# Where a diffusion backbone's modulation products run: other stages of a two-layer kernel, one pass for the context, and two steps of side work a piece at two places

## The chip, the cores and the metric

The kernel runs on one core of one Trainium2 chip. A core has engines that run side by side: TensorE (PE: matmuls, with its weight loads as PEld), VectorE (DVE), ScalarE (ACT), GpSimd (POOL) and SyncE (SP), which here only issues transfers. Transfers run on 16 DMA engines. The metric is the device time of one execution in microseconds; lower is better.

## What is computed

Two layers over 256 latent tokens (x) and 256 context tokens (ctx), width 1024, fp32. The core of the reference, cut:

```python
mod   = silu(c) @ w_mod[l] + b_mod[l]          # latents
mod_c = silu(c_ctx) @ w_mod[l] + b_mod[l]      # context
sh1, sc1, ga1, sh2, sc2, ga2 = split(mod, 6)   # and the same six of mod_c
h  = rms_norm(x, g_pre_mix[l]) * (1 + sc1) + sh1      # hc from xc with mod_c
(mq, mk, mv, mo, mg, aq, ak, av, nq, nk, nv, zg) = split(h @ w_in[l])   # and from hc
y_ml = mlstm_branch(...)     # both directions, starts from the context's state
y_ga = gqa_latent(...)       # rotary, keys of context and latents
y_na = na_latent(...)        # neighbourhood window, plus the context
o = sum over branches of sigmoid(zg) * (y @ w_branch) @ w_out[l]
x = x + ga1 * rms_norm(o, g_post_mix[l])
f = conv_ffn(rms_norm(x, g_pre_ffn[l]) * (1 + sc2) + sh2, w_up, conv, w_down)
x = x + ga2 * rms_norm(f, g_post_ffn[l])
# in layer 0 the context takes the same path; in layer 1 it only gives keys, values and states
```

The six vectors sh1, sc1, ga1, sh2, sc2, ga2 are called keys below. In layer 0 each has two streams, latents and context; in layer 1 only sh1 and sc1 have both.

## The kernel before, in words

**Weights come in pieces.** The program is a list, `self.prog`, of pieces. A `Raw` is one transfer of 512 KB from memory into one of five raw tiles, issued on SP's queue in the order of use (`dma` in `run`, line 190); a raw tile comes free when its piece has been split or used. A weight piece is split before use (lines 208 and 209): ScalarE copies it to `whi` in a rounded format, VectorE subtracts to get `wlo`. `mm3` (line 307) then makes three matmuls, high by high, high by low, low by high. Splits run up to two pieces ahead. `block` cuts a projection into pieces of two 128-row slices (24 matmuls of 512 columns in layer 0; latents alone, in layer 1, take 24 of 256 or 12 of 512); `down_block` makes one-slice pieces for `w_out` and `w_down`.

**Side work.** Attention and mLSTM are Python generators in the queue `self.side`. After each piece `run` calls `step` as often as the piece's `side` says, once by default: a generator emits its instructions up to its next `yield`. So side work stands between weight pieces in every engine's order, and all engines execute in that order. `finish(key)` and `drain` emit, without pieces between, whatever a generator has left; a piece's `need` calls them where a result is wanted. The generators: `g_na` (neighbourhood attention; 14 steps in layer 0, 10 in layer 1), `g_gqa` (2 steps of tables and norms, 7 of rotary work, then 14 or 10 of attention), `g_gates` (5 steps), `g_mlstm` (2 steps, then four heads, each scores with the weighting product, an empty step and the outputs; it emits empty steps while the flags `mready` or `vready` are not set) and `g_mlfin` (waits for `oready`, then normalises the heads and transposes them, line 1075). In an attention step (`g_attend`) stand the PV product of the unit before last (line 701), the transposes of the last unit (687) and the scores of this one (648, 651), with VectorE's and ScalarE's softmax between.

**The order of a layer's mixer** (`layer`, line 1090 on): nq, in layer 1 the first NA gate, nk, nv, keys and values (kv), queries (q), the NA gates (in layer 1 the GA gates too), the NA projection (needs `na`), in layer 0 the GA gates, mk, in layer 0 the GA projection (needs `gqa`), mq, mv, in layer 1 the GA projection, the first ML gate, mo, the second ML gate, the ML projection (needs `drain`). Then `w_out`, norms, the FFN's eleven up blocks with convolution taps on VectorE (1308), and the down blocks.

**Modulation.** sc1 and sh1 of layer 0 are made by matmuls at the start. All other keys are made by `mod_dot` (line 424): each of eight pieces per key brings a transposed weight block of 128 outputs by 1024 inputs and VectorE multiplies it with the broadcast vector `CB` and sums along the row (line 440, `scalar_tensor_tensor` with `accum_out`). The latents take one operation over 1024 columns, which writes its products back over the raw tile. The context takes two over 512 columns, which write into the scratch tile `jnk` and leave two half sums to be added at the key's end (line 450). These pieces have `side=0`, no split and no matmul. `mod_end` adds the bias and gains. `spread` (line 482) puts such pieces at even distances among the pieces from a place to the program's end. Before, ga1, sh2, sc2, ga2 of layer 0 and sh1 of layer 1 (40 two-stream pieces) are spread over layer 0's mixer from nv on, and sc1, ga1, sh2, sc2, ga2 of layer 1 (8 two-stream and 32 one-stream pieces) over layer 0's FFN, ups from the third block on and both downs, 80 pieces. The dots between the first ML gate and the ML projection of layer 0 get `side=1`.

## Time and profile before

| | |
|---|---|
| median of 3 runs | 1533.33 us (1532.9 to 1535.78) |
| the profiled execution | 1536.47 us, of which the span is 1534.7 us |
| mean granted TensorE clock | 0.983 |
| busy: PE, PEld, DVE | 1451.6, 1251.6, 1089.4 us |
| busy: ACT, POOL | 731.4, 214.9 us |
| transfers | 238.08 MB, mean 155 GB/s |

The span is the time from the first to the last instruction. A group line of the profile names a source line, an engine, an operation and its tiles (out<-in), then count, busy time and mean duration. A waits line gives the total waiting time, how often, and the longest wait. A line of the timeline has start and duration in us and, in brackets, the idle time before it and what ended it. Matmuls overlap each other in the records, so a busy TensorE isn't TensorE at its peak: how many matmuls stand in a stretch tells more. Stages of the span: start to about 50 us, layer 0's mixer to about 570, `w_out` and norms to 661, ups to about 846, downs to about 973, layer 1's mixer to about 1310, then its FFN.

### The profile page before, as it was taken

Reading aid. Unit: us, or ns where it says so; the run is one execution under the profiler, and the core shown is the slowest. Engines: PE = TensorE matmul, PEld = TensorE weight load, DVE = VectorE, ACT = ScalarE, POOL = GpSimd, SP = SyncE. Lnnn points to the kernel's source line nnn. Section 1 sums busy time; section 2 is a strip of 40 time slices with the busy share of each in tenths; the row PEclk is TensorE's granted clock in tenths of the full one; section 3 lists DMA queues with packets and bytes.
Section 4 is the critical chain, followed back from the end, with each engine's and each line's share of the span. In section 5 each row is a group of like instructions: output and inputs, shape, how many; then the busy total and the mean of one; then the engine's idle time right before and its main releaser. Section 6 shows DMA issues by size and latency. Waiting matters only on the chain.

```text
span 1534.7 us, 23004 instructions
## 1 busy us (share of the span) xinstructions
PE 1451.6 (95%) x8689; PEld 1251.6 (82%) x8689; DVE 1089.4 (71%) x1974; ACT 731.4 (48%) x1343; POOL 214.9 (14%) x318
## 2 busy tenths in 40 slices
PE   6999998998999799899999999999999999799997
PEld 3877787776888688888888887887888898699986
DVE  3548787777755788888766888636885356678874
ACT  4334441543436347634434564635554455566663
POOL 2000012002412031111111000000110330202100
PEclk9999999999999999999999999999999999889999
DMA  9624344231544356454545787732442444445662
GB/s 336 215 87 140 110 138 128 93 110 56 158 145 119 122 191 195 153 163 141 161 164 165 245 282 247 248 99 84 146 127 69 110 112 163 146 146 186 214 201 92
DMA packets 103807, 238.08 MB, mean 155 GB/s; under 512 B 8416, under 2 KB 18720, under 8 KB 103568
## 3 DMA queue, kind: packets, MB, share of 16 engines
q1 hardware_dynamic: 99472, 224.56, 45.7%
q0 software_dynamic: 4224, 12.05, 3.0%
q8 instruction: 68, 1.11, 0.3%
q14 instruction: 43, 0.35, 0.1%
HBM read 235.50 MB, written 1.08 MB: 154 GB/s over the span
## 4 chain that ended last, share of the span: by engine, by line
PE 70%; DVE 16%; ACT 5%; issue 4%; DMA 4%; POOL 1%; DVEq 0%; SPq 0%; ACTq 0%; POOLq 0%
PE bank L307 58%; DVE wlo L209 4%; DMA raw<-in_w_down 3%; PE bank L687 2%; PE bank L651 2%; PE bank L701 2%; DVE ta L1308 1%; ACT whi L208 1%; DVE jnk L440 1%; DVE D L999 1%; ACT D L982 1%; DVE raw L440 1%; PE bank L648 1%; DMA raw<-in_w_mod 1%; PE bank L409 1%
## 5 line engine op out<-in xcount | busy, mean ns | idle before, releaser
L209 DVE TENSOR_TENSOR wlo<-raw,whi 128x1024 fp32r<-128x1024 f32 (+1 forms) x330 | 411.1, 1260 | 163.4 <-ACT whi L208 162.4
L307 PE MATMUL bank<-HThi,whi 128*128 128x256 f32 (+1 forms) x1408 | 466.0, 331 | 9.9 <-DVE sig L1161 2.9
L307 PE MATMUL bank<-HThi,wlo 128*128 128x256 f32 (+1 forms) x1408 | 461.1, 327 | 7.4 <-DVE wlo L209 7.4
L307 PE MATMUL bank<-HTlo,whi 128*128 128x256 f32 (+1 forms) x1408 | 460.8, 327 | 0.5 <-DVE HTlo L570 0.5
L208 ACT CAST whi<-raw 128x1024 fp32r<-128x1024 f32 (+1 forms) x330 | 336.0, 1038 | 212.3 <-PE bank L307 73.0
L307 PEld LDWEIGHTS bank<-HThi,whi 128*128 128x128 f32 x1408 | 270.6, 192 | 41.7 <-issue 16.2
L307 PEld LDWEIGHTS bank<-HThi,wlo 128*128 128x128 f32 x1408 | 270.7, 192 | 27.4 <-DVE wlo L209 8.9
L307 PEld LDWEIGHTS bank<-HTlo,whi 128*128 128x128 f32 x1408 | 270.8, 192 | 19.0 <-DVE HTlo L570 1.2
L307 PE MATMUL bank<-whi,xs 128*128 128x512 f32 x528 | 161.4, 383 | 2.0 <-DVE o L602 1.1
L1308 DVE SCALAR_TENSOR_TENSOR ta<-bank,cw,ta 128x255 f32<-128x255 f32 (+2 forms) x224 | 110.7, 527 | 53.7 <-ACT ta L1305 49.7
L307 PE MATMUL bank<-whi,HThi 128*128 128x512 f32 (+1 forms) x384 | 143.4, 373 | 0.3 <-DVE sig L1161 0.2
L307 PE MATMUL bank<-wlo,HThi 128*128 128x512 f32 (+1 forms) x384 | 139.9, 364 | 0.8 <-DVE wlo L209 0.8
L307 PE MATMUL bank<-whi,HTlo 128*128 128x512 f32 (+1 forms) x384 | 139.6, 364 | 0.0
L307 PEld LDWEIGHTS bank<-whi,xs 128*128 128x128 f32 x528 | 100.7, 191 | 18.5 <-DVE o L602 1.5
L307 PE MATMUL bank<-wlo,xs 128*128 128x512 f32 x264 | 101.6, 385 | 4.5 <-DVE wlo L209 4.5
L440 DVE SCALAR_TENSOR_TENSOR raw<-raw,CB 128x1024 f32<-128x1024 f32 x80 | 102.0, 1275 | 1.7
L663 ACT ACTIVATE pr<-bank,mn 128x512 f32<-128x512 f32 (+1 forms) x96 | 58.4, 614 | 91.7 <-DVE mn L660 85.3
L1328 POOL TENSOR_TENSOR hT<-ta 128x256 f32<-128x256 f32 (+1 forms) x48 | 59.1, 1232 | 305.8 <-ACT ta L1327 305.5
L1305 ACT ACTIVATE ta<-bank,cw 128x256 f32<-128x256 f32 (+1 forms) x96 | 61.0, 645 | 85.5 <-PE bank L307 84.0
L307 PEld LDWEIGHTS bank<-whi,HThi 128*128 128x128 f32 x384 | 73.0, 190 | 21.6 <-issue 11.6
L307 PEld LDWEIGHTS bank<-wlo,HThi 128*128 128x128 f32 x384 | 73.0, 190 | 9.6 <-DVE wlo L209 1.5
L307 PEld LDWEIGHTS bank<-whi,HTlo 128*128 128x128 f32 x384 | 72.9, 190 | 8.7
(231 smaller groups left out, 1805.1 us busy)
## 6 DMA issues: line engine op xcount, KB each, us to landing
raw<-in_w_in SPq DMA_DIRECT2D x112, 512.0 KB, 3.8
raw<-in_w_up SPq DMA_DIRECT2D x96, 512.0 KB, 4.6
raw<-in_w_modT SPq DMA_DIRECT2D x80, 512.0 KB, 4.5
raw<-in_w_down SPq DMA_DIRECT2D x66, 512.0 KB, 4.7
raw<-in_w_branch SPq DMA_DIRECT2D x24, 512.0 KB, 3.6
raw<-in_w_out SPq DMA_DIRECT2D x24, 512.0 KB, 4.2
raw<-in_w_mod SPq DMA_DIRECT2D x16, 512.0 KB, 10.6
nab<-in_nabias POOLq DMA_DIRECT2D x16, 256.0 KB, 3.2
```

Of the source, the lines that this page charges most:

```text
L208: nc.scalar.copy(p.hi, src)
L209: nc.vector.tensor_tensor(p.lo, src, p.hi.bitcast(F32), op=ALU.subtract)
L307: nc.tensor.matmul(out, l, self.woven(r), start=first and i == 0, stop=last and i == 2)
L409: nc.tensor.matmul(st["b"][32 * g:32 * g + 32, 256 * ch:256 * ch + 256], w, rt[:, g, :], start=c == 0, stop=c == 1)
L440: nc.vector.scalar_tensor_tensor(o, rt[:, 0, a:b], 1.0, self.CB[:, s, a:b], op0=ALU.mult, op1=ALU.mult, accum_out=acc)
L651: nc.tensor.matmul(b, q[:, c0:c0 + 128], k[:, 0:512], start=True, stop=True)
L663: nc.scalar.activation(out=pt[:, w * i:w * i + w], in_=b[:, w * i:w * i + w], func=ACTF.Exp, scale=-1.0, bias=mn[:, i:i + 1], accum_out=mn ...
L687: nc.tensor.transpose(b[:, o:o + 128], pt[:, 128 * i:128 * i + 128], self.I)
L701: nc.tensor.matmul(b[64 * par:64 * par + 64, 0:w], v_of(p, par, kt), pTs[par][:, w * kt:w * kt + w], start=kt == 0, stop=kt == nkt - 1)
L1305: nc.scalar.activation(out=tv, in_=bv, func=ACTF.Identity, scale=cw[:, ch, 1:2], bias=cw[:, ch, 3:4])
L1308: nc.vector.scalar_tensor_tensor(o, x, cw[:, ch, t:t + 1], o, op0=ALU.mult, op1=ALU.add)
L1328: nc.gpsimd.tensor_tensor(hv, av, ta, op=ALU.mult)
```

## The change

One pass for the context: `jnk` becomes a bf16 tile of 1024 columns, and each stream takes one operation over 1024 columns that writes its products there; the half sums and their addition go. `spread` gets an end. The keys' places change: in layer 0's mixer ga1 between nk and the end of q, sh2 and sc2 from there to the end of the GA projection; beside layer 0's ups (third block on) ga2 of layer 0, sh1 and sc1 of layer 1; in layer 1's mixer ga1 and sh2 between nq and the end of nv, sc2 and ga2 from the end of mk to the second ML gate. Nothing is spread over layer 0's downs any more. The NA projection of layer 0 gets two steps a piece. In both layers mo moves ahead of the first ML gate, and the four pieces before mo (mv in layer 0, the GA projection in layer 1), mo itself and the first ML gate get two steps a piece.

```diff
-        self.jnk = self.const([128, 512], name="jnk")
+        self.jnk = self.const([128, 1024], BF16, name="jnk")
...
-                def dot(o, a, b, s, acc):
-                    nc.vector.scalar_tensor_tensor(o, rt[:, 0, a:b], 1.0, self.CB[:, s, a:b], op0=ALU.mult, op1=ALU.mult,
-                                                   accum_out=acc)
-                if len(streams) == 2:
-                    if j == 0:
-                        st["h"] = self.sm([128, 8], name="mh")
-                    dot(self.jnk, 0, 512, 1, dst[:, j, 1:2])
-                    dot(self.jnk, 512, 1024, 1, st["h"][:, j:j + 1])
-                dot(rt[:, 0, :], 0, 1024, 0, dst[:, j, 0:1])
+                for s in streams:
+                    nc.vector.scalar_tensor_tensor(self.jnk, rt[:, 0, :], 1.0, self.CB[:, s, :], op0=ALU.mult, op1=ALU.mult,
+                                                   accum_out=dst[:, j, s:s + 1])
                 if j == 7:
-                    if len(streams) == 2:
-                        nc.vector.tensor_tensor(dst[:, :, 1], dst[:, :, 1], st["h"], op=ALU.add)
...
-    def spread(self, first, pieces):
+    def spread(self, first, last, pieces):
-        body = self.prog[first:]
+        body, rest = self.prog[first:last], self.prog[last:]
         del self.prog[first:]
...
-        self.prog += pieces[at:]
+        self.prog += pieces[at:] + rest
...
         in_nat("nv", C_NV, [0, 1, 2, 3], ev_v("nv"), after=lambda: self.add_side(self.g_na(l), "na"))
+        valued = self.prog[-1]
         self.block(cols(C_A, 272), 8, 272, "nat", [0, 1, 2, 3], X, ev_kv)
...
+        attend = self.prog[-1]
...
         proj(NA, 0, need=lambda: self.finish("na"))
         if L0:
+            for p in self.prog[-4:]:
+                p.side = 2
             zg(GA, 0)
             zg(GA, 1)
...
+        mlstm = self.prog[-1]
         in_T("mq", C_MQ, lat_all, None, after=ready("mready"))
...
         first = len(self.prog)
+        in_nat("mo", C_MO, tl, ev_mo, after=ready("oready"))
         zg(ML, 0)
-        in_nat("mo", C_MO, tl, ev_mo, after=ready("oready"))
         zg(ML, 1)
+        for p in self.prog[first - 4:first + 8]:
+            p.side = 2
...
         if L0:
-            self.spread(p0 + 8, [p for k in KEYS[2:] for p in self.mod_dot(0, k)] + self.mod_dot(1, KEYS[0]))
-            for p in self.prog[self.prog.index(first):self.prog.index(stop)]:
-                p.side = 1
+            a, b = self.prog.index(attend), self.prog.index(mlstm)
+            self.spread(a, b, [p for k in ("sh2", "sc2") for p in self.mod_dot(0, k)])
+            self.spread(p0 + 6, a, self.mod_dot(0, "ga1"))
+        if not L0:
+            self.spread(self.prog.index(mlstm), self.prog.index(stop), [p for k in ("sc2", "ga2") for p in self.mod_dot(1, k)])
+            self.spread(p0 + 2, self.prog.index(valued), [p for k in ("ga1", "sh2") for p in self.mod_dot(1, k)])
...
             for blk in range(2, 11):
                 up(blk, (0, 512))
+            self.spread(f0 + 16, len(self.prog), [p for l1, k in ((0, "ga2"), (1, "sh1"), (1, "sc1")) for p in self.mod_dot(l1, k)])
...
-            self.spread(f0 + 16, [p for k in KEYS[1:] for p in self.mod_dot(1, k)])
```

## The prediction

> **What bounds the kernel now.** I read the page first, then the waits of TensorE, then busy times by stage, then single stretches of the chain of waits and the timeline.

> ```profile
> span 1534.7 us, 23004 instructions
> ...
> PE 1451.6 (95%) x8689; PEld 1251.6 (82%) x8689; DVE 1089.4 (71%) x1974; ACT 731.4 (48%) x1343; POOL 214.9 (14%) x318
> ...
> PE 70%; DVE 16%; ACT 5%; issue 4%; DMA 4%; POOL 1%; DVEq 0%; SPq 0%; ACTq 0%; POOLq 0%
> ```

> TensorE carries the kernel, so moving VectorE work shortens nothing by itself: only stretches in which TensorE waits can shrink. The stages show where that is (columns: PE busy, with the number of matmuls; PEld, DVE, ACT, POOL; granted clock; DMA share; GB/s).

> ```profile
> 204.60:261.80 57.20, 52.70 (x243) 45.37 (x241) 47.58 (x103) 16.22 (x25) 15.06 (x14) 0.94 0.45 140
> 343.40:364.10 20.70, 14.40 (x75) 8.02 (x73) 15.13 (x37) 9.18 (x31) 0.52 (x1) 0.84 0.15 52
> ...
> 503.50:536.80 33.30, 25.36 (x114) 21.34 (x113) 25.11 (x62) 11.41 (x25) 0.00 (x0) 0.90 0.38 127
> ...
> 661.00:838.00 177.00, 176.71 (x819) 154.79 (x820) 135.05 (x178) 71.94 (x87) 26.28 (x18) 1.00 0.49 157
> 838.00:893.00 55.00, 53.66 (x245) 45.56 (x244) 43.39 (x61) 27.81 (x42) 3.34 (x2) 1.00 0.72 239
> 893.00:961.00 68.00, 62.86 (x290) 52.97 (x289) 57.39 (x91) 39.52 (x72) 2.15 (x6) 0.97 0.76 261
> ```

> The up projections of layer 0 (661 to 838 us) run at full speed: 177 us for 819 matmuls, 0.216 us each. That figure prices the others: 245 matmuls would take 52.9 of the 55.0 us behind them, 290 would take 62.6 of 68.0, 114 would take 24.6 of 33.3 (a little less each, as a few are short transposes). The biggest holes are 343 to 364, 503 to 537 and 893 to 961.

> **What a dot costs.** A dot is one weight block's inner products for one key.

> ```profile
> L440 DVE SCALAR_TENSOR_TENSOR jnk<-raw,CB x96: 679/691/1781, 70.7 to 729.8; 128x512 f32<-128x512 f32 x96
> ...
> L440 DVE SCALAR_TENSOR_TENSOR raw<-raw,CB x80: 1209/1224/1837, 72.2 to 967.5; 128x1024 f32<-128x1024 f32 x80
> ```

> With two streams it takes 2 x 0.691 + 1.224 = 2.6 us of VectorE now and 2 x 1.224 = 2.45 us after; with one stream 1.22 us. No VectorE row writes bf16 from two f32 inputs; a price for the new output lies between 0.69 us (a halved op) and 1.38 us (two half ops), and I take 1.22, the row of the same inputs. The one add at a key's end goes; the other small operations there move with the key and lie beside TensorE as the dots do. All dots now write the same scratch tile, in VectorE's own order, and leave the raw tile as it was. The change moves 16 two-stream dots (ga2 of layer 0 and sh1 of layer 1) out of layer 0's mixer, leaving 24; puts 24 two-stream dots beside the 36 up pieces that had 18 dots; empties both down stages; and gives layer 1's mixer 32 one-stream dots, each with its 512 KB load on SP's queue.

> **Layer 0, attention.** The 23 grouped-attention steps are four short of cover: the branch projection (GA) forces what is left at once, from 343.4 to 364.1. The same steps under cover:

> ```profile
> 334.96 5.38 PE bank L307 x24
> 340.34 1.02 PE bank L701 x16
> 341.37 1.02 PE bank L687 x8
> 342.39 1.07 PE bank L648 x8
> ```

> A weight piece is 5.38 us and a step beside it adds 1.02 + 1.02 + 1.07. The forced stretch holds four PVs, three transposes and two scores: 4 x 1.02 + 3 x 1.02 + 2 x 1.07 = 9.3 us of work in 20.7. Two steps a piece on the four NA projection pieces supply exactly the four missing steps, so the 11.4 us go: **-11.4**. The price is at those pieces. They hold the rotary steps, and VectorE is already late there.

> ```profile
> PE bank L307 <- DVE sig L1161: 4.5, 2, 2.9
> ```

> Doubling the steps puts four more rotary steps on VectorE and GpSimd in some 22 us, and VectorE, in order, waits for GpSimd's product before it can write the rotated query that the next TensorE transpose reads. The splits of the next two pieces were queued before, which hides one piece, 5.4 us. Bounds: -8 (today's 4.5 and a slow-clock stretch vanish) to +6; nearest is today's row, so I take a third more, **+1.5**.

> **Layer 0, mLSTM.** With mo ahead of both ML gates and two steps a piece, the last head and the finish end a stage earlier, and no dots stand in VectorE's queue. Six steps on the first three mv pieces find nothing to do.

> ```profile
> 519.28 1.04 PE L1075 MATMUL bank<-ident,H 128*128 128x128 f32 x4 [5.20 <-DVE H L1070]
> 522.35 1.09 PE L1075 MATMUL bank<-ident,H 128*128 128x128 f32 x4 [2.03 <-DVE H L1070]
> ```

> TensorE waits 5.20 + 2.03 = 7.2 us for the normalised heads; two dots (5.2 us) stand in front of them. Without these 2.0 remain, and the slow-clock stretch that follows is gone:

> ```profile
> 519.40:526.10 6.70, 4.67 (x15) 3.76 (x15) 6.60 (x13) 2.12 (x3) 0.00 (x0) 0.50 0.23 78
> ...
> 1285.20:1289.00 3.80, 0.38 (x4) 0.19 (x3) 3.54 (x12) 0.00 (x0) 0.00 (x0) 1.00 0.42 138
> ```

> 6.7 us at 0.50 cost half, 3.4. Together **-8.6**, of the 8.7 lost in this stretch. The order of mo and the first gate itself costs nothing: the same pieces stand beside the same steps.

> **Layer 0, FFN.** Ups: VectorE 135 us less 8 x 2.6 + 10 x 1.22 is 102; 24 x 2.45 brings it to 161 of 177. Full cover by TensorE, so 0; if the cover goes, see the rivals. Downs: 2.1 + 5.4 = 7.5 us lost, where half of all pieces brought a second 512 KB and 1.22 us; without them the wait for a norm chain (ScalarE squares, GpSimd root, then VectorE) stays, some 0.5: **-7**.

> **Layer 1, start.** Sixteen dots go among thirteen pieces, eight of them ahead of nk, which needs the context's norm. VectorE there:

> ```profile
> 988.20 1.67 DVE L510 TENSOR_SCALAR xn<-x,nr 128x512 f32<-128x512 f32 x4 [6.55 <-POOL nr L126]
> 989.79 4.62 DVE L209 TENSOR_TENSOR wlo<-raw,whi 128x1024 fp32r<-128x1024 f32 x4
> 998.10 0.43 DVE L569 CAST HThi<-ht 128x512 fp32r<-128x512 f32 x1 [3.69 <-ACT ht L566]
> ```

> Eight dots are 9.8 us. Two fall into the 6.55 us hole, six (7.3) stand between the splits and the casts, where 3.69 us are free: 3.6 us later, **+3.6**. From 0 (all in holes) to +9.8 (none). Loads: six weight blocks and eight dots, five of them fetched ahead, are nine blocks of 512 KB in six pieces of 2.7 us, 290 GB/s, above the 261 of the downs; a late load is part of that upper end. SP's queue issues in the order of use, and a dot holds one of the five raw tiles until VectorE has read it.

> **Layer 1, gates and mLSTM.** A dot (1.22) may stand ahead of the gate scan, for which TensorE waits already: **+1.2** (0 to 4).

> ```profile
> PE bank L1075 <- DVE H L1070: 3.4, 1, 3.4
> PE bank L902 <- DVE B L897: 1.2, 1, 1.2
> ...
> PE bank L307 <- DVE wlo L209: 0.8, 1, 0.8
> ```

> The two-step pieces (GA projection, mo, first ML gate) are short here, 256 columns, and this is the dear place. One head:

> ```profile
> 1236.38 3.29 PE L1010 MATMUL bank<-mv,D 128*128 128x129 f32 x28
> ...
> 1249.28 3.29 PE L1010 MATMUL bank<-mv,D 128*128 128x129 f32 x28
> ```

> ```profile
> 1244.31 2.94 ACT L208 CAST whi<-raw 128x1024 fp32r<-128x1024 f32 x3
> ...
> 1246.51 2.47 DVE L999 TENSOR_TENSOR D<-D,bank 128x256 f32<-128x256 f32 x8
> ```

> The two fences are TensorE's outputs of two heads, and ScalarE and VectorE between them. From output to output are 12.9 us, three pieces among them. The chain inside (output, ScalarE's exponentials to 1244.3, a weight split, VectorE's product to 1249.0) takes 12.6, so three pieces just fill it; where no split stands between, 7.9 + 2.47 = 10.4. With two steps a piece only two, one and two pieces remain between the four heads. A piece of 256 columns is half of 5.38, 2.7 us: TensorE has 10.2, 7.5 and 10.2 us of work against 12.6, 10.4 and 12.6, which makes waits of 2.4, 2.9 and 2.4; with about today's 3.4 at the end 11.1, and with one slow-clock stretch (half of 3.4) 12.8. Today's waits there are 3.4 and 0.8: **+8.6**, from 0 (the chain is shorter than one head shows) to +15 (a slow-clock stretch behind each wait). The pieces not spent there run behind it with nothing beside them. One-stream dots fall into VectorE's holes before the product, as its first operation waits for ScalarE.

> [...] This trace shows 0.94 in the stretch from 204.6, whose longest wait is 2.9 us, and 1.00 after the 3.4 us wait that fills the stretch from 1285.2: the length alone does not decide. [...]

> **Sum.** -11.4 + 1.5 - 8.6 - 7 + 3.6 + 1.2 + 8.6 = -12.1 us. The profiled execution took 1536.47 us (1.8 outside its span of 1534.7), 3.1 above the median of 1533.33; taken off both, it gives 1524.4 and **1521.2**. The sum stands on the profiled execution's rows alone; that the median shrinks by the same amount is assumed.

> **Rivals.** *VectorE bounds the ups* (slower). Its place is 661 to 838; it decides from the mean dot op at which 102 + 48 ops exceed 177, 1.56 us. For it: both forms reach 1.8 us (1781, 1837), beside GpSimd's work, which the ups have. Against: the medians. At 1.84 the sum is 190, 13 us over, and nine blocks each with half a 3.4 us slow stretch add 15: 1521.2 + 28 = 1549. [...]

> *The attention steps only change places*: the rotary steps stall the NA projection for as long as the end saves: 1521.2 + 11.4 = 1532.6, no change. For it: VectorE 47.58 of 57.2 there already. Against: those steps hold hardly any TensorE work.

> *Layer 1 hides everything*: its 3.6 + 1.2 + 8.6 us are not paid: 1507.8. For it: VectorE is busy only half of layer 1's mLSTM. Against: the 12.6 us chain.

> **Chances.** Forecast 0.66, VectorE in the ups 0.08, steps change places 0.13, layer 1 free 0.13. The forecast's own bounds (start +6, mLSTM +8, gates +3 one way, layer 1 the other) make 1508 to 1534, which holds the second and third rival too; the range is 1505 to 1534. This kernel's measurement tells 0.2%, 3 us, from no change. Faster: forecast, free layer 1 and a little of the third, 0.79; same 0.11; slower 0.10.

> **What would show it.** Right: no forced steps ahead of the GA projection and 8.5 us pieces through mk; a wait of 2 us at L1075 in layer 0; ups still at 0.216 us a matmul with VectorE near 0.9; downs with DMA near 200 GB/s; new waits at L1010 in layer 1. Wrong: gaps between up pieces; a wait over 8 us at the NA projection; nk of layer 1 late by over 8 us; or layer 1's heads still 12.9 us apart with TensorE full.

## The result, and the profile after

The changed kernel is slower: 1543.64 us median (1541.85 to 1545.4, 8 runs) against 1535.13 of 8 runs of the kernel before, a ratio of 1.0057 with a 95% interval of 1.0044 to 1.007. That is 8.7 us more where 12.1 less was forecast, outside the range and of the other sign. Below, every "us below" or "above before" is the ratio of the runs, less one, times 1535; the whole time beside it is the median.

The page of the changed kernel, first its span, then busy time, then the shares of the chain that ended last:

```profile
span 1543.6 us, 22952 instructions
...
PE 1459.3 (95%) x8689; PEld 1262.2 (82%) x8689; DVE 1077.0 (70%) x1872; ACT 732.7 (47%) x1343; POOL 214.3 (14%) x318
...
PE 80%; DVE 10%; ACT 4%; issue 3%; DMA 2%; POOL 1%; DVEq 0%; SPq 0%; POOLq 0%; ACTq 0%
```

The same 8689 matmuls take 7.7 us more of TensorE, although VectorE has 12.4 us less to do. Equal matmuls that take longer point to a lower clock (0.975 in the mean for 0.983), and in the kernel before the clock was low where TensorE waited (0.84 from 343.4 to 364.1 us); so the next view is that of stages. Busy times by stage of the changed kernel (columns as in the prediction): layer 0's ups from 661 us on, its downs, layer 1's start, then layer 1's mLSTM from its gates to the end of the ML projection:

```profile
661.00:826.60 165.60, 165.60 (x769) 145.02 (x768) 146.64 (x185) 67.15 (x82) 27.83 (x16) 1.00 0.52 168
826.60:945.80 119.20, 118.08 (x561) 102.73 (x561) 84.11 (x116) 72.01 (x122) 6.34 (x8) 1.00 0.60 195
945.80:1034.40 88.60, 74.30 (x403) 66.29 (x401) 47.37 (x70) 28.71 (x51) 4.11 (x9) 0.88 0.59 189
1193.80:1317.00 123.20, 110.88 (x742) 103.47 (x741) 80.66 (x181) 55.28 (x117) 25.86 (x46) 0.93 0.57 173
```

The same last three stages in the kernel before:

```profile
844.00:972.00 128.00, 121.52 (x560) 103.02 (x559) 107.34 (x162) 72.00 (x122) 5.49 (x8) 0.99 0.78 261
972.00:1040.70 68.70, 66.01 (x402) 59.52 (x401) 28.62 (x37) 28.93 (x51) 4.12 (x9) 1.00 0.44 140
1199.00:1308.60 109.60, 103.63 (x741) 97.55 (x741) 64.53 (x148) 55.73 (x117) 26.81 (x46) 0.98 0.46 128
```

Layer 0 went as forecast in sum: at the start of its downs the changed kernel is 17.3 us ahead (844.0 to 826.6), at their end 26.2. The ups run full. Layer 1 takes it back and more: its start is 19.9 us longer (88.60 for 68.70), its mLSTM 13.6 (123.20 for 109.60). The start shows two halves: TensorE idles 14.3 us where it idled 2.7, and with a clock of 0.88 the same matmuls take 74.30 us where they took 66.01.

TensorE waits there for the context's normalised input (`HThi`, needed by nk) and for split weights; total, times, longest from 945.8 to 1034.4 us:

```profile
PE bank L307 <- DVE HThi L560: 6.3, 1, 6.3
PE bank L307 <- DVE wlo L209: 5.4, 3, 3.9
PE bank L307 <- ACT whi L208: 2.6, 3, 1.6
```

VectorE makes both in one order, with idle time of its own between, so what lies behind is seen on the queues. First the longest waits of ScalarE, then of SP's queue, from 945.8 to 1000 us of the changed kernel:

```profile
ACT whi L208 <- DMA raw<-in_w_in: 34.1, 6, 9.1
```

```profile
SPq L190 <- DVE wlo L209: 20.0, 8, 5.3
SPq L190 <- DVE jnk L439: 17.2, 9, 6.0
```

ScalarE waits for weights to land, and the queue that would fetch them waits for VectorE to let go of a raw tile. Three timelines of the changed kernel, SP's queue, ScalarE and VectorE, show the circle:

```profile
968.81 0.38 SPq L190 DMA_DIRECT2D raw<-in_w_in  x1
969.96 0.33 SPq L190 DMA_DIRECT2D raw<-in_w_modT  x1
975.84 0.38 SPq L190 DMA_DIRECT2D raw<-in_w_in  x1
976.98 0.33 SPq L190 DMA_DIRECT2D raw<-in_w_modT  x1
```

```profile
973.51 1.04 ACT L208 CAST whi<-raw 128x1024 fp32r<-128x1024 f32 x1 [9.10 <-DMA raw<-in_w_in]
979.86 1.04 ACT L208 CAST whi<-raw 128x1024 fp32r<-128x1024 f32 x1 [5.30 <-DMA raw<-in_w_in]
```

```profile
974.59 1.22 DVE L209 TENSOR_TENSOR wlo<-raw,whi 128x1024 fp32r<-128x1024 f32 x1 [4.66 <-ACT whi L208]
980.93 1.22 DVE L209 TENSOR_TENSOR wlo<-raw,whi 128x1024 fp32r<-128x1024 f32 x1 [3.98 <-PE bank L307]
```

A weight transfer is issued at 968.81, its block can be split at 973.51, the split ends at 975.81, and at 975.84 the next weight transfer is issued: one weight block in 7.0 us, for a piece with 2.7 us of work. From 949 to 1009 us eleven weight transfers go out, one per 6.0 us. The addresses in the program show why: the blocks issued at 956.49, 968.81, 975.84 and 982.19 go into one and the same raw tile, each when the split of the one before has let go of it, and the other four tiles hold dots. In layer 0's downs, the dots of the kernel before had not done this. Its SP queue there:

```profile
926.75 0.33 SPq L190 DMA_DIRECT2D raw<-in_w_modT  x1
927.90 1.80 SPq L190 DMA_DIRECT2D raw<-in_w_down  x2
931.96 0.33 SPq L190 DMA_DIRECT2D raw<-in_w_modT  x1
```

One dot for two pieces lets two weight transfers go out together. Sixteen dots among thirteen pieces leave one at a time.

### The profile page after: what moved, and what is told of

Its sections match the earlier page's. It is cut to its first block, busy times and chain, and to the rows that moved or that the text cites. A ratio compares the mean times of both kernels' runs of the same rounds, so it can differ in the third digit from the quotient of the medians.

```text
span 1543.6 us, 22952 instructions
## 1 busy us (share of the span) xinstructions
PE 1459.3 (95%) x8689; PEld 1262.2 (82%) x8689; DVE 1077.0 (70%) x1872; ACT 732.7 (47%) x1343; POOL 214.3 (14%) x318
## 4 chain that ended last, share of the span: by engine, by line
PE 80%; DVE 10%; ACT 4%; issue 3%; DMA 2%; POOL 1%; DVEq 0%; SPq 0%; POOLq 0%; ACTq 0%
PE bank L307 66%; PE bank L678 3%; PE bank L692 3%; PE bank L642 2%; DVE wlo L209 2%; PE bank L1001 2%; DVE ta L1312 1%; DMA raw<-in_w_in 1%; ACT whi L208 1%; ACT D L973 1%; DVE jnk L439 1%; PE bank L639 1%; PE bank L409 1%; DMA raw<-in_w_mod 1%; PE bank L980 1%
## 5 line engine op out<-in xcount | busy, mean ns | idle before, releaser
L209 DVE TENSOR_TENSOR wlo<-raw,whi 128x1024 fp32r<-128x1024 f32 (+1 forms) x330 | 408.2, 1248 | 188.7 <-ACT whi L208 183.8
L307 PE MATMUL bank<-HThi,whi 128*128 128x256 f32 (+1 forms) x1408 | 469.1, 333 | 14.7 <-DVE HThi L560 8.0
L307 PE MATMUL bank<-HThi,wlo 128*128 128x256 f32 (+1 forms) x1408 | 464.3, 330 | 10.9 <-DVE wlo L209 10.7
L307 PE MATMUL bank<-HTlo,whi 128*128 128x256 f32 (+1 forms) x1408 | 463.7, 329 | 0.2 <-DVE HTlo L561 0.2
L208 ACT CAST whi<-raw 128x1024 fp32r<-128x1024 f32 (+1 forms) x330 | 337.2, 1037 | 256.0 <-PE bank L307 112.5
L307 PEld LDWEIGHTS bank<-HThi,whi 128*128 128x128 f32 x1408 | 273.7, 194 | 47.3 <-issue 14.9
L307 PEld LDWEIGHTS bank<-HThi,wlo 128*128 128x128 f32 x1408 | 273.5, 194 | 31.3 <-DVE wlo L209 12.8
L307 PEld LDWEIGHTS bank<-HTlo,whi 128*128 128x128 f32 x1408 | 273.5, 194 | 19.0 <-DVE HTlo L561 1.0
L439 DVE SCALAR_TENSOR_TENSOR jnk<-raw,CB 128x1024 bf16<-128x1024 f32 x128 | 167.5, 1309 | 1.7
L307 PE MATMUL bank<-whi,xs 128*128 128x512 f32 x528 | 159.9, 381 | 0.9 <-DVE ta L1312 0.8
L307 PE MATMUL bank<-whi,HThi 128*128 128x512 f32 (+1 forms) x384 | 143.4, 373 | 0.5 <-DVE sig L1152 0.5
L307 PE MATMUL bank<-wlo,HThi 128*128 128x512 f32 (+1 forms) x384 | 139.8, 364 | 0.0
L307 PE MATMUL bank<-whi,HTlo 128*128 128x512 f32 (+1 forms) x384 | 139.6, 364 | 0.0
L307 PEld LDWEIGHTS bank<-whi,xs 128*128 128x128 f32 x528 | 99.8, 189 | 16.6 <-ACT ta L1331 1.3
L307 PE MATMUL bank<-wlo,xs 128*128 128x512 f32 x264 | 100.2, 379 | 0.3 <-DVE wlo L209 0.3
L307 PEld LDWEIGHTS bank<-whi,HThi 128*128 128x128 f32 x384 | 73.0, 190 | 21.2 <-issue 11.5
L307 PEld LDWEIGHTS bank<-whi,HTlo 128*128 128x128 f32 x384 | 73.0, 190 | 8.8
L307 PEld LDWEIGHTS bank<-wlo,HThi 128*128 128x128 f32 x384 | 73.1, 190 | 8.1
```

What stands on the lines that cost most here:

```text
L208: nc.scalar.copy(p.hi, src)
L209: nc.vector.tensor_tensor(p.lo, src, p.hi.bitcast(F32), op=ALU.subtract)
L307: nc.tensor.matmul(out, l, self.woven(r), start=first and i == 0, stop=last and i == 2)
L439: nc.vector.scalar_tensor_tensor(self.jnk, rt[:, 0, :], 1.0, self.CB[:, s, :], op0=ALU.mult, op1=ALU.mult, accum_out=dst[:, j, s:s + 1])
```

## The experiments

Seventeen kernels ran, in five groups; a group shares its runs of the kernel before. Theory 1 of the start is the circle above; its rivals are VectorE's time, which the prediction had counted, and the DMA engines' throughput.

**First group: where layer 1 loses.** The first run gives the dots of layer 1's start a free slot of the pool `u` when three are free (10 of the 16 get one).

```diff
-                if r.early and self.free:
+                if r.early and len(self.free) >= r.early:
...
+            raw = Raw(..., 1, 1024, 3 if l == 1 and key in ("ga1", "sh2") else False)
```

> The changed kernel, but the 16 dots at the start of layer 1 load into free slots of another pool when it has three, so that they rarely hold one of the five raw tiles. Nothing is left out. The changed kernel is 8.5 us above the kernel before; its layer 1 start lost 20 us. Theory 1 (a dot holds a raw tile until its turn, so weight blocks are fetched one at a time and their 4.4 us to landing shows): 10 to 17 us of the 20 come back, so 2 to 9 us below the kernel before. Rival 2 (VectorE's time for the dots): no change, 8 us above. Rival 3 (the DMA engines move no more than this): no change, 8 us above.

Measured: 1526.78 us, ratio 0.9953 (0.9938 to 0.9969): 7.2 us below before. Layer 1's start:

```profile
944.40:1015.70 71.30, 67.12 (x402) 60.97 (x400) 46.70 (x70) 28.85 (x51) 4.12 (x9) 0.98 0.62 209
```

Of the 19.9 us, 17.3 are back, with VectorE as busy as in the changed kernel (46.70 for 47.37) and with more bytes moved per us (209 GB/s for 189). So neither of these was at its limit. TensorE's wait for `HThi` falls from 6.3 to 1.0 us, so it too came from the late weights, whose splits stand ahead of those casts on VectorE.

The second leaves the loads and takes VectorE's time out: `jnk`, the raw tile and `CB` are cut to 32 columns in the dots of ga1 and sh2 of layer 1, so the rest of these inner products is left out.

> The changed kernel, but the 16 dots at the start of layer 1 multiply only 32 of their 1024 columns (the rest of these inner products is left out); their loads, their raw tiles and their places stay. VectorE has some 16 x 1.1 = 18 us less to do there. Theory 1 (raw tiles): at most 3 us come back, 5 to 9 us above the kernel before. Rival 2 (VectorE's time): 10 to 18 us come back, 2 to 10 us below the kernel before. Rival 3 (DMA bandwidth): no change, 8 us above.

Measured: 1540.64 us, 1.004 (1.0025 to 1.0056), 6.1 above before; the start:

```profile
941.60:1029.90 88.30, 72.54 (x404) 64.50 (x402) 30.93 (x70) 28.79 (x51) 4.11 (x9) 0.88 0.58 190
```

VectorE is 16.4 us less busy and the stage is 0.3 us shorter (the whole kernel, by its runs, 2.6). VectorE's time falls as the main cause of the start.

The third takes the second step away in layer 1 only:

```diff
-        for p in self.prog[first - 4:first + 8]:
+        for p in self.prog[first - 4:first + 8] if L0 else ():
```

> The changed kernel with one step of side work a piece in layer 1's mLSTM (two stay in layer 0); mo stays ahead of the ML gates, the 16 late dots stay. Layer 1's mLSTM lost 13.6 us in the changed kernel. Theory (two steps a piece leave the chain of a head uncovered and bare pieces behind it): 9 to 13 us come back, 1 to 5 us below the kernel before. Rival (the late dots among those pieces make the loss): at most 3 us come back, 5 to 9 us above.

Measured: 1538.06, 1.003 (1.0017 to 1.0043), 4.6 above before: about 4 came back, between theory and rival.

The fourth moves the late dots:

```diff
-            self.spread(self.prog.index(mlstm), self.prog.index(stop), [... ("sc2", "ga2") ... self.mod_dot(1, k)])
...
+            self.spread(d0, len(self.prog), [p for k in ("sc2", "ga2") for p in self.mod_dot(1, k)])   # d0: start of the downs
```

> The changed kernel with layer 1's 16 late one-stream dots (sc2, ga2) among layer 0's 44 down pieces instead of beside the mLSTM; two steps a piece stay. In the downs one dot for 2.75 pieces, where the kernel before had one for two and lost 7.5 us: they give back 2 to 4 us of the 9 gained there. Theory (two steps): the mLSTM gains at most 3 us, so 8 to 12 us above the kernel before. Rival (late dots): the mLSTM gains 9 to 13, so 0 to 4 us above the kernel before.

Measured: 1538.66, 1.0029 (1.0014 to 1.0045), 4.5 above. In the trace the downs give back 4.1 us, the mLSTM is 118.9 us long for 123.2. Both steps and late dots cost something in the mLSTM; neither theory alone holds.

**Second group: steps and late dots apart.** The first adds own slots (as in the first experiment) and moves sc2's dots between the ends of q and mk, ga2's into layer 1's ups; the second has one step as well.

> The first experiment (dots of layer 1's start in own slots, 7 us below the kernel before) with the late dots away from the mLSTM: sc2's 8 between the end of the attention projection and the end of mk, ga2's 8 among layer 1's up pieces; two steps a piece stay. Nothing is left out. From the run with the late dots in the downs: the mLSTM gains 5.5 us, and the new places cost 0 to 3. Theory (late dots cost the mLSTM 5.5): 9.5 to 12.5 us below the kernel before. Rival (that gain was the profile's scatter, some 3 us between equal stretches): 5 to 8 below.

> The same as the one above with one step a piece in layer 1's mLSTM. Theory (two steps and late dots cost the mLSTM separately, 4.1 and 5.5 us): 13 to 17 us below the kernel before, some 4 below the one above. Rival (the two steps cost only together with dots in VectorE's queue): the same as the one above within 1.5 us.

Measured: 1527.68, 0.9956 (0.9941 to 0.9971), 6.8 below, where the rival had put it; and 1520.96, 0.991 (0.9879 to 0.994), 13.8 below. The mLSTM of the two, and then that of the best kernel of the third group, which is coded like the second here:

```profile
1179.60:1300.30 120.70, 110.45 (x742) 103.50 (x741) 64.47 (x148) 56.36 (x117) 24.88 (x46) 0.93 0.41 116
```

```profile
1181.30:1293.70 112.40, 106.28 (x742) 100.09 (x741) 64.63 (x148) 55.74 (x117) 26.88 (x46) 0.95 0.43 125
```

```profile
1174.90:1283.00 108.10, 101.98 (x742) 96.30 (x741) 64.56 (x148) 55.77 (x117) 26.86 (x46) 1.00 0.45 130
```

Without any dot beside them, two steps a piece cost 8.3 us between the first two, 4.1 of it idle time of TensorE (120.70 less 110.45, against 112.40 less 106.28) and the rest clock; by the runs it is 7.0. The idle part agrees between executions, the clock's part does not: the third row has the same 6.1 us idle and is 4.3 shorter, and the two other one-step kernels without late dots there (own slots for more dots, and one step on the NA projection, both below) show 110.0 and 114.5 us. Both kernels lose 4.6 us in layer 1's attention and gates (163.1 us for 158.5), where sc2's dots now stand; that ate what the first gained.

The third shortens the late dots to 32 columns at their old places (the rest of these inner products is left out), the fourth offers them own slots (4 of 16 get one).

> The changed kernel with the 16 late dots of layer 1 multiplying 32 of their 1024 columns (the rest of these inner products is left out); loads, raw tiles, places and two steps stay. Theory (a late dot stands in VectorE's queue ahead of the head's product and of the normalisation): 4 to 6 us come back, 2.5 to 4.5 above the kernel before. Rival (raw tiles held, weights late): at most 1 comes back, 7.5 to 9 above.

> The first experiment with the late dots of layer 1 in free slots of the other pool as well, where it has three free; full length, two steps. Theory (VectorE's queue): no change to the first experiment, 6 to 8.5 us below the kernel before. Rival (raw tiles): 4 to 6 us more, 11 to 13.5 below.

Measured: 1535.48, 1.0011 (0.9997 to 1.0026), 1.7 above, so 7.0 came back when VectorE's time was taken out; the trace shows 5.0 of it in the mLSTM (118.2 us for 123.2) and 1.7 just ahead (158.0 for 159.7), where the first two late dots stand. The fourth: 1524.82, 0.9933 (0.9914 to 0.9952), 10.3 below, but its mLSTM is no shorter than in the first experiment; with 4 slots of 16 it settles nothing.

**Third group: parts of the change alone, and better versions.** The first two are the kernel before with one edit: `side = 2` on the last four pieces of layer 0's NA projection; and the dots as the change has them.

> The kernel before with one part of the change alone: two steps of side work on the four pieces of layer 0's NA projection. Forecast from the prediction's two terms (-11.4 for the forced attention steps, +1.5 for the rotary steps): 9.9 us below the kernel before, and the trace of the changed kernel gave 9.8 at this place. Rival (the steps only change places): no change, within 2 us.

> The kernel before with one part of the change alone: both streams' dots in one pass of 1024 columns each, with a bf16 scratch tile. VectorE saves 0.15 us at each of 56 two-stream dots. Theory (VectorE is not what TensorE waits for where the dots are): within 2 us of the kernel before. Rival (the downs are late for VectorE): 3 to 6 us below.

Measured: 1531.31, 0.9977 (0.9964 to 0.9989), 3.5 below, not 9.9; and 1530.44, 0.9968 (0.9957 to 0.998), 4.9 below, priced at nothing in the prediction (and not in the downs, where the rival looked for it: 128.6 us for 128.8). The profiled execution of the first was its fastest (1525.67 us). It shows 9.0 us at the end of the attention, but about 5 of that is half-clock time that the profiled execution of the kernel before had and this one had not: a clock of 0.94 over 57.2 us and 0.84 over 20.7 are 6.7 us, against 0.97 over 58 us and 1.00 in the end stretch, 1.7. One profiled execution against another gave the wrong size here; the runs together decide.

The other two build on the run with one step: own slots offered to sc2's and ga2's dots too; and sc2's dots among layer 0's downs instead.

> The run with the late dots spread and one step a piece in layer 1 (14 us below the kernel before), with own slots for the dots of sc2 and ga2 too, where three are free. The attention lost some 3.7 us there and layer 1's up pieces 1.6. Theory (these are weight blocks that wait for raw tiles held by dots): 3 to 5 us more, 17 to 19 below the kernel before. Rival (VectorE's time in the attention): no change, 13 to 15 below.

> As the one above, but sc2's 8 dots among layer 0's 44 down pieces, in the common raw tiles. The downs with 16 dots gave back 4.0 us; with 8, one for 5.5 pieces, 0.5 to 2. Theory (own slots make the attention free): 15 to 18 below the kernel before, no better than the one above. Rival (VectorE's time in the attention): 16 to 18 below, 2 to 4 better than the one above.

Measured: 1519.87, 0.9899 (0.9884 to 0.9914), 15.5 below, between theory and rival; and 1514.32, 0.9864 (0.9846 to 0.9882), 20.9 below, the best of all and more than either had expected. The attention still loses 4.6 us in the first (3 of sc2's 8 dots got a slot), and 0.1 in the second. Which of the dots' two effects costs it there stays open; away from the attention they cost the downs 1.6 us (120.8 for 119.2).

**Fourth group: what two steps on the NA projection are worth.** The best kernel with one step there, and the kernel before with both parts.

> The best run so far (sc2 in the downs, own slots, one step in layer 1's mLSTM; 20.9 us below the kernel before) with one step a piece on layer 0's NA projection, as in the kernel before. Theory A (two steps there are worth what the kernel before with them alone measured, 3.9 us): 16 to 18 us below the kernel before. Theory B (they are worth the 9.9 us of the prediction, and the other run was short of it because two-stream dots in two passes stood beside them): 10 to 12 below.

> The kernel before with the two parts together: dots in one pass, and two steps a piece on layer 0's NA projection. Theory A (they add up: 4.7 + 3.9): 7.5 to 10 us below the kernel before. Theory B (the passes stand in VectorE's queue beside the doubled steps, so that the steps bring their 9.9 only once the passes are shorter): 13 to 15 below.

Measured: 1517.67, 0.9883 (0.9858 to 0.9908), 18.0 below, so the steps bring 2.9 in the best kernel; and 1527.48, 0.9951 (0.9935 to 0.9967), 7.5 below, so they bring 2.6 on top of one pass. Theory A holds, at 2.6 to 3.5 us with the run of the steps alone; the pair of best kernels would not show it by itself, as the intervals of its 4 and 6 runs overlap. The best kernel first with one step (NA projection, then the end of the attention), then with two:

```profile
204.00:262.00 58.00, 57.59 (x276) 49.24 (x275) 51.81 (x103) 18.39 (x31) 16.31 (x14) 1.00 0.48 145
340.00:362.00 22.00, 17.72 (x82) 11.86 (x82) 12.88 (x32) 9.67 (x26) 3.58 (x15) 0.84 0.17 50
```

```profile
204.00:262.00 58.00, 52.69 (x256) 42.55 (x254) 51.06 (x106) 18.75 (x35) 13.12 (x14) 0.94 0.36 115
```

With fewer and shorter dots TensorE is full at the NA projection (57.59 of 58); doubling the steps brings 5.3 us of idle time there and a clock of 0.94 (another 3.5), about what the forced stretch loses (4.3 idle, and 0.16 x 22 = 3.5 of clock). That is why little is left of the 11.4: the GA projection starts at 352.4 us with two steps and at 354.9 with one, 2.5 us apart.

**Fifth group: the raw tiles themselves.** The number of raw tiles, and as control the room alone that seven take.

```diff
-        self.p_raw = mk("raw", 5)
+        self.p_raw = mk("raw", 7)      # RB = 7; six in the other run
-        self.p_t = mk("t", 14)
+        self.p_t = mk("t", 10)         # 12 with six
```

> The changed kernel with six raw tiles instead of five; the room comes from the pool of 512-column work tiles, 12 instead of 14. Nothing else. Theory 1 (layer 1's start loses 20 us because dots hold the raw tiles): one tile more lets a weight block be fetched ahead, so a large part comes back, 6 to 14 us, between 5.5 below and 2.5 above the kernel before; VectorE's and the DMA's theory: none of it, 7 to 10 above.

> The same with seven raw tiles, and 10 work tiles. Theory 1: layer 1's start within 5 us of the kernel before's, so 4 to 9 us below the kernel before, as with own slots. If raw tiles held by the 16 late dots cost the mLSTM too, 3 to 5 us more, 9 to 13 below; if those cost VectorE's time only, no more.

> The changed kernel with five raw tiles and 10 work tiles: the price of the room alone. Expected: no change to the changed kernel, 7 to 10 us above the kernel before; if work tiles are short, up to 10 us more, which is then to be added to what the two runs above gained.

Measured: six tiles 1531.4, 0.9984 (0.9972 to 0.9996), 2.5 below before; seven 1527.61, 0.9958 (0.9946 to 0.997), 6.4 below; five with the small pool 1543.15, 1.0061 (1.0038 to 1.0084), 9.4 above. Layer 1's start and mLSTM with six tiles, then with seven:

```profile
943.40:1022.20 78.80, 70.64 (x402) 63.60 (x400) 47.20 (x70) 28.91 (x51) 3.88 (x9) 0.91 0.66 214
1181.50:1303.60 122.10, 109.12 (x741) 101.69 (x741) 81.20 (x181) 56.13 (x117) 25.04 (x46) 0.94 0.56 175
```

```profile
943.90:1019.20 75.30, 68.97 (x404) 62.28 (x402) 46.85 (x70) 29.09 (x51) 3.35 (x8) 0.95 0.66 220
1178.60:1300.90 122.30, 110.60 (x742) 103.39 (x741) 80.97 (x181) 56.47 (x117) 25.46 (x46) 0.93 0.57 175
```

The start falls from 88.6 to 78.8 and 75.3 us, while the mLSTM stays at 122: raw tiles are the cause of the first loss and of little or nothing of the second.

## Why the prediction was wrong

**Layer 1, start: forecast +3.6 (0 to +9.8), measured +19.9. This step failed.** It priced sixteen dots as VectorE's time in VectorE's holes. VectorE's time costs 0.3 us there (short dots, by the trace). The prediction named the true resource in its last sentence, "a dot holds one of the five raw tiles until VectorE has read it", and then checked the loads as throughput (290 GB/s against the 261 seen). The stage as a whole came to 189 GB/s. What counts is how many weight blocks can be on their way. Weights give their tile back when they are split, up to two pieces ahead; a dot keeps its tile until its own turn, and all transfers are issued in the order of use. With a dot for every piece, four of the five tiles fill with dots and one weight block at a time is on its way: 6.0 us a block on average, 7.0 in the circle shown above. The 261 GB/s row stood for one dot in two pieces and could not be carried over to a denser stage. Half-clock time, 8.3 of the 19.9 us, came on top of the idle time. The sign that the prediction named for this case, "nk of layer 1 late by over 8 us", came: counted from the stage's start, nk is 17.8 us late.

**Layer 1, gates and mLSTM: forecast +1.2 and +8.6, measured +1.1 and +13.6.** The gates' term was right in size, and it goes when the late dots are shortened or moved (158.0 and 158.6 us for 158.5). Two steps alone cost 8.3 us in the traces and 7.0 by the runs, near the forecast 8.6, but put together differently and so in part by luck: 4.1 of idle time where 6.9 were forecast (11.1 less the 4.2 of the kernel before), and the clock took more than the 1.7 given to it (half of 3.4 us; the kernel before has a clock of 0.50 there from 1205.43 to 1208.84 us, the changed kernel 0.93 over 123.20). TensorE's waits in the mLSTM with two steps and no dots there, then the longest with one step (total, times, longest):

```profile
PE bank L1066 <- DVE H L1061: 4.7, 1, 4.7
PE bank L1001 <- DVE D L990: 4.1, 4, 2.1
PE bank L893 <- DVE B L888: 1.2, 1, 1.2
```

```profile
PE bank L1066 <- DVE H L1061: 3.3, 1, 3.3
```

What failed is "One-stream dots fall into VectorE's holes": late dots cost 2.5 us beside two steps (123.2 against 120.7; 4.3 against the 118.9 with them in the downs) and 6.7 beside one (119.1 against 112.4). Of the 2.5 and the 6.7, 2.1 and 4.4 are idle time of TensorE; the rest is clock, which differs between executions of equal code. VectorE's timeline in the changed kernel, between the last head and its normalisation, for which TensorE waits 5.8 us (4.7 without the dots):

```profile
1270.94 1.22 DVE L439 SCALAR_TENSOR_TENSOR jnk<-raw,CB 128x1024 bf16<-128x1024 f32 x1
...
1272.43 1.23 DVE L209 TENSOR_TENSOR wlo<-raw,whi 128x1024 fp32r<-128x1024 f32 x1 [0.27 <-ACT whi L208]
1273.58 1.22 DVE L439 SCALAR_TENSOR_TENSOR jnk<-raw,CB 128x1024 bf16<-128x1024 f32 x1
...
1274.72 1.22 DVE L209 TENSOR_TENSOR wlo<-raw,whi 128x1024 fp32r<-128x1024 f32 x1
1275.86 0.17 DVE L117 TENSOR_SCALAR rs_a<-ssH 128x8 f32<-128x8 f32 x1
```

VectorE took its instructions in the order written: ScalarE's last sum for the normalisation ended at 1271.5, and the normalisation stood behind two dots, the first just begun, and two splits until 1275.86. The prediction had seen just this in layer 0 (two dots in front of the heads) and not looked for it here.

**Layer 0, attention: forecast -9.9, in the trace -9.8, and right by accident.** Two steps on the NA projection are worth 2.6 to 3.5 us by the runs, because the price there, in the best kernel against the same kernel with one step, is not +1.5 but 8.4 (5.3 idle and 3.5 of clock, against 0.4). The kernel before already lost 8.0 at that place (4.5 idle, and 0.06 x 58 of clock), so against it the price hardly shows. The rest came from a term put at nothing: shorter and fewer dots in layer 0's mixer, which would have freed this place. One pass alone gives 4.9 us; its trace shows 3.9 between the neighbourhood attention and the gates. That "moving VectorE work shortens nothing by itself" was wrong where VectorE ends the last wait, and the 4.5 us wait quoted for the NA projection was such a place: with one pass it is 3.9, and the clock there 1.00 for 0.94.

**Layer 0, mLSTM: forecast -8.6, measured -5.9** from the gates to the start of the up stage. The wait for the heads fell from 7.2 to 3.8 us, not to 2.0, and a half-clock stretch still follows it (0.50 from 490.56 to 497.39 us). **Ups: forecast 0, measured 0**; they ran full, with dots at the forecast time, and the rival that VectorE would bound them did not come:

```profile
L439 DVE SCALAR_TENSOR_TENSOR jnk<-raw,CB x128: 1211/1219/2322, 62.7 to 1306.1; 128x1024 bf16<-128x1024 f32 x128
```

The bf16 output costs nothing (1.219 us for 1.224), and the dot takes no longer than the split's subtraction of the same shape (1.22 us), before and after. **Downs: forecast -7, measured -8.8.**

So layer 0's terms sum to -25.5 forecast and -24.5 measured (1.7 more came ahead of its attention), and the sign turned in layer 1, whose terms sum to +13.4 forecast and +34.6 measured. The bounds were no help: the upper end of the start's range, +9.8, was again VectorE's time.

## What to carry to other kernels

In layer 1's start a load that rode in a shared ring of buffers cost what it held, not what it moved (with own slots 17.3 of the 19.9 us came back, at 209 GB/s for 189): count, in the order of use, how many of the critical transfers can be in flight while every slot waits for its turn, and set the circle of issue, landing and release against the time of a piece. A one-stream dot among layer 0's down pieces cost 0.20 us at one in 5.5 pieces (1.6 for 8) and 0.26 at one in 2.75 (4.1 for 16); at more than one for each piece of layer 1's start it cost 1.24 (19.9 for 16), and 0.41 there with two raw tiles more (6.6 for 16). And a dot put "into a hole" of VectorE's order was paid where the next critical operation was written behind it (TensorE waited 5.8 us for the normalisation with dots in front of it, 4.7 without): look at what stands in front of each short chain that TensorE waits for, in both layers. With dots kept out of the attention and the mLSTM, own slots and one step a piece in layer 1, the same change gives 1514.32 us, 20.9 less than before.

## What the hardware showed that was not expected

```profile
1238.08:1241.49 3.41, 1.66 (x12) 1.26 (x10) 3.41 (x10) 0.40 (x1) 2.30 (x4) 1.00 0.65 214
1241.49:1244.91 3.42, 3.27 (x16) 3.10 (x15) 3.39 (x9) 0.00 (x0) 1.50 (x3) 0.50 0.50 53
```

```profile
1258.28:1261.70 3.42, 1.68 (x16) 1.49 (x14) 3.04 (x15) 1.17 (x2) 0.00 (x0) 1.00 0.50 150
1261.70:1265.11 3.41, 1.82 (x16) 1.82 (x17) 3.38 (x6) 1.12 (x2) 0.00 (x0) 1.00 0.03 11
```

A window that was little more than half idle (1.66 of 3.41 us busy) was enough in the changed kernel. That window and the two of the best lie close together, 0.49, 0.49 and 0.53 busy, with different outcomes; what decides so near the middle stays open. A stall's size is uncertain by as much again, and two profiled executions of equal code lie several us apart: layer 1's mLSTM with one step and no late dots has 6.1 to 6.5 us idle in four kernels and takes from 108.1 to 114.5 us.
